# A transformer trunk on one core: another beat for the attention pairs beside the gate sums, and other sizes for the modulation sums

## The chip, the core and the metric

The kernel runs on one core of a Trainium2 chip. Its engines work side by side and wait for each other only by semaphores: TensorE (PE in the profile; PEld is its loading of weights), VectorE (DVE), ScalarE (ACT), GpSimd (POOL) and SyncE (SP), which starts most transfers. The metric is the device time of one execution in microseconds (us), lower being better.

## The reference

One layer of a hybrid backbone, in fp32, on 128 context tokens and 256 latent tokens of width 2048 (16 heads of 64):

```python
def trunk_layer(x, cond, lw, attend):
    ...
    sh1, sc1, g1, sh2, sc2, g2 = modulation(cond, w_mod_l, b_mod_l)
    h = rms_norm(x, n1) * (1 + sc1) + sh1
    q, k, v, u = project_in(h, w_in_l, qg_l, kg_l)
    attn = attend(q, k, v)
    x = x + g1 * token_mixing(h, attn, u, w_na_proj_l, w_fnet_proj_l, w_gate_l, w_o_l)
    h2 = rms_norm(x, n2) * (1 + sc2) + sh2
    x = x + g2 * swiglu(h2, w_gu_l, w_down_l)
    return x, k, v

def modulation(cond, w_mod, b_mod):
    m = jax.nn.silu(cond) @ w_mod + b_mod
    return jnp.split(m[..., None, :], 6, axis=-1)

def token_mixing(h, attn, u, w_na_proj, w_fnet_proj, w_gate, w_o):
    ...
    na = attn.reshape(b, t, D_NA) @ w_na_proj
    fn = fourier_mix(u) @ w_fnet_proj
    g_na, g_fn = jnp.split(jax.nn.sigmoid(h @ w_gate), 2, axis=-1)
    return (g_na * na + g_fn * fn) @ w_o
```

Context tokens attend to themselves; latent tokens attend in one softmax to a window of their grid and to 128 cached keys. `fourier_mix` is the real part of a 2-D DFT over positions and group channels.

## The kernel before

All large products are made in three passes: a number is split into a rounded part H and a rest L, and `mm3` issues H x H, H x L and L x H (lines 145 to 147; for the weights, `split` casts H on ScalarE at line 141 and subtracts L on VectorE at line 142). Weights come in units of 2 x 128 rows by 512 columns. `next_unit` hands PE the next unit, splits the unit two later, and lets side work advance. Nothing is scheduled by the compiler: every engine runs its instructions in the order in which the code writes them.

Side work is written as generators under `Paced`: one `yield` is one step, a rate says how many steps a tick takes. The list `behind` gets one tick per weight unit; the list `front` gets three, two in `next_unit` and one in `mid_unit`, which is called in the middle of a unit, between its second and third slice of 128 features.

The stages that matter here:

1. Input projection (512-wide matmuls). The modulation sums `mod_sums` make shift and scale of the first norm: `MODS` lists sums as (first k-tile, number n of k-tiles), each of 8 steps whose matmuls (line 402, 128 x n columns wide) take four column groups of PE at once; then `mod_cols` turns the rows into columns (line 418), and `modulate` makes H and L of each of these k-tiles of the layer's input (`hH`, `hL`). Their weights `wm` have four buffers. The projection goes through groups of k-tiles, `GROUPS` = 1, 2, 4 and 9, each over all eight column blocks, and needs a k-tile's `hH` and `hL` when its group starts on it. `PREP` are the rates of the modulation work in each group, `DUE` its first advance. When the modulation is through, `rows` begins: the other modulation rows, added up on VectorE (`accr`, line 327).
2. Gate sums (384-wide matmuls): eight sums `fc8`, each of 8 weight units with four accumulators of 128 features. After the last unit, each accumulator is copied out into `gst` (line 1029), and the four are stored by ScalarE's queue (line 1032). Beside them, three ticks a unit, `front` runs the Fourier part and then attention, eight pairs of heads. One pair's ticks are the fields of `PAIR`, divided by commas: qk transposes queries and keys and splits them; b adds the mask to the bias; s0 and s1 are the scores of each half of the queries, m their maxima, e the exponentials, i the reciprocals and scalings, t the transposes of the probabilities, v the split of the values, pv the product with the values of the pair before; lq, lv, lb load the next pair's data. A sum has 24 ticks, a pair 15.
3. Gate products, output projection, feed-forward.

The accumulators (PSUM) are two pools of four tiles: `mm` and `at`. `acc_tile` takes them from a ring of seven, three of `at` and four of `mm`; side work takes `at` tiles (after the output projection, `mm` tiles) beside the ring. `new_ring` starts it anew, last before the gate products.

Ahead of the change, the copy of the first two accumulators goes to VectorE where one of the last three ticks had exponentials, else to ScalarE:

```python
(nc.vector.tensor_copy if f < 2 and any(soft) else nc.scalar.copy)(st, po[f][:, :TOK])
```

Of the kernel before, what the change touches and what calls it, by code (L numbers as in the profile page):

```python
# [29 lines left out]
TOK = CTX + LAT  # L30
# [5 lines left out]
HALF = NL + NC  # L36


MODS = [(0, 1), (1, 3), (4, 3), (7, 3), (10, 3), (13, 3)]
GROUPS = [(0, 1), (1, 2), (3, 4), (7, 9)]  # L40
ORDER = [6, 7, 0, 1, 2, 3, 4, 5]
DUE = [-1.4, 0, 0, 0]
PREP = [1.75, 1.8, 1.8, 1.8]
PAIR = "qk,b,pv,s0 m0,e0 i0,lq,s1 m1,e1 i1,,t0 lb,v,,t1,lv,"

# [52 lines left out]
def trunk_kernel(ctx: ExitStack, tc: tile.TileContext, io: dict):  # L100
    nc = tc.nc
# [89 lines left out]
    front, behind = [], []  # L191
# [10 lines left out]
    def mid_unit():  # L202
        for p in front:
            p.tick()
# [59 lines left out]
    with ExitStack() as ph:  # L264
# [3 lines left out]
        def mm_tile():  # L268
            return ps.tile([P, CH], F32, tag="mm", name=nm("mm"))
# [3 lines left out]

        ring = None

        def new_ring():

            nonlocal ring
            ring = itertools.cycle([at_tile] * 3 + [mm_tile] * 4)

        def acc_tile():

# [87 lines left out]
        def depth_of(n):  # L370

            return 4 if n == 1 else 2

        def mod_weights(alloc):
# [12 lines left out]

            return Ahead(load, [(kt0, n, k0) for kt0, n in MODS for k0 in range(0, KT, depth_of(n))], 0)

        def mod_sums(src, kt0, n, alloc, out):  # L390


            w, nk = n * P, depth_of(n)
            pm = at_tile()
            for k0 in range(0, KT, nk):
                _, wm = src.take()
                for kk in range(0, nk, 2):
                    for ty in range(2):
                        for par in range(2):
                            k = k0 + kk + par  # L400
                            q = 32 * (2 * ty + par)
                            nc.tensor.matmul(  # L402
                                pm[q : q + 32, :w], csz[:, k, :], wm[:, ty, kk + par, :],
                                start=k < 2, stop=k >= KT - 2, tile_position=(0, q), skip_group_check=True,
                            )
                    if kk + 2 >= nk:
                        src.more()
                    if k0 + kk + 2 >= KT:
                        rows = alloc([P, w], "mrow")
                        nc.scalar.copy(rows, pm[:, :w])  # L410
                        out.append(rows)
                    yield
# [22 lines left out]
        with ExitStack() as pha:  # L435
# [117 lines left out]
            sums = []  # L553
            for i, _ in enumerate(mod_sums(src, *MODS[0], wme, sums)):
                if i in (1, 3, 5):
# [5 lines left out]
            def columns_and_tokens(k0, n):  # L561
                yield from mod_cols(k0, n, sums.pop(0))
                for kt in range(k0, k0 + n):
                    modulate(kt)
                    prepared[0] = kt + 1
                    yield

            def prepare():

                follow = columns_and_tokens(*MODS[0])  # L570
                while prepared[0] < 1:
                    yield next(follow)
                for k0, n in MODS[1:]:
                    for _ in mod_sums(src, k0, n, wme, sums):
# [75 lines left out]
            for gi, (k0, n) in enumerate(GROUPS):  # L650
                prep.due, prep.rate = DUE[gi], PREP[gi]
                if gi == len(GROUPS) - 1:
                    behind.append(Paced(expand_rpb()))
                    new_ring()
                for rate, ci in zip(CHUNKS, ORDER):
                    if gi == len(GROUPS) - 1:
                        rows.rate = rate
                    po = [(mm_tile if gi < len(GROUPS) - 1 else acc_tile)() for _ in range(NT)]
# [35 lines left out]
        def fourier():  # L694
            with ExitStack() as st:
# [60 lines left out]
                    i = slice(4 * pair + cp, 4 * pair + cp + 3, 2)  # L756
                    split(fHs[:, i], fLs[:, i], f)

                for _ in range(6):
                    yield  # L760
                lat = table([P, 2, 2 * NL], io["dft_lat"].rearrange("(t p) n -> p t n", p=P))
                ctx_ = table([P, 256], io["dft_ctx"])
# [47 lines left out]
                values()  # L810

        qks, vs, biases = [], [], []
        soft = deque(maxlen=3)

        def load_qk(hp):
            ci, co = hp // 4, (hp % 4) * P
# [26 lines left out]
        def attention_pair(hp, wk, values_before):  # L843
# [152 lines left out]
            }  # L996
            for tick in PAIR.split(","):
                for w in tick.split():
                    work[w]()
                soft.append("e" in tick)  # L1000
                yield
            return values

# [11 lines left out]
        for fc8 in range(8):  # L1015
            po = [mm_tile() for _ in range(4)]
            sts = []
            for u in range(0, KT, 2):
                wH, wL = next_unit()
                for f in range(4):  # L1020
                    s = slice(f * P, (f + 1) * P)
                    if f == 2:
                        mid_unit()
                    for kk in range(2):
                        k = u + kk
                        mm3(po[f][:, :TOK], wH[:, kk, s], wL[:, kk, s], hH[k], hL[k], k == 0, k == KT - 1)
                    if u == KT - 2:
                        st = gst.tile([P, TOK], F32, tag="st", name=nm("gst"))
                        (nc.vector.tensor_copy if f < 2 and any(soft) else nc.scalar.copy)(st, po[f][:, :TOK])  # L1029
                        sts.append(st)  # L1030
            for f, st in enumerate(sts):
                nc.scalar.dma_start(s_gate[fc8][:, f], st)
# [36 lines left out]
                    gates.more()  # L1069
                yield  # L1070

        new_ring()
        for f4 in range(4):
            gl = [None, None]
            for i, bH, bL in ((1, fH, fL), (0, aH, aL)):
                _, gl[i] = gates.take()
                po = [acc_tile() for _ in range(4)]
# [84 lines left out]
    for cc in range(4):  # L1162
        xin[cc] = tmp.tile([P, NT, CH], F32, tag="xin", name=nm("xin"))
        behind.append(Paced(load_residual(cc)))
        po = [acc_tile() for _ in range(NT)]
# [121 lines left out]
    for part, nf in enumerate(FF_PARTS):  # L1287
# [5 lines left out]
        for c4 in range(nf // 4):  # L1293
            for half in (1, 0):
                po = [acc_tile() for _ in range(4)]
# [35 lines left out]
        for cc in range(4):  # L1331
            po = [acc_tile() for _ in range(NT)]
# [72 lines left out]
```

## Time and profile before

| | |
|---|---|
| median of three runs | 2059.26 us (2057.69 to 2059.97) |
| the profiled execution | 2057.84 us, its span 2056.0 us |
| PE busy | 2030.4 us, 99% of the span |
| VectorE, ScalarE busy | 1247.9 us (61%), 758.2 us (37%) |
| moved by DMA | 390.46 MB, mean 190 GB/s |
| granted clock of TensorE | 0.998 |

Busy time of PE counts a matmul from its start to its modelled end, and matmuls overlap: two 384-wide ones start 0.17 us apart and last 0.33 each. So PE reads as busy where it is slowed down, and its stalls are found in the list of waits and in distances between matmuls. In a timeline, the columns are start, length, engine, line, operation, tiles written and read, count, and in brackets the idle time before with what ended it. In the list of waits they are engine, tile and line that waited, what for, and then total us, times, and the longest. The input projection runs until about 330 us, the gate sums until about 683, gate products until about 815, the output projection until about 950.

### The profile page before, as it was taken

To read this page: it belongs to the slowest core of one execution; us is meant where nothing else is said; L and a number is where in the kernel's file an instruction comes from. 1 tells how busy PE (TensorE), PEld (TensorE's weight loads), DVE (VectorE), ACT (ScalarE), POOL (GpSimd) and SP (SyncE) were. 2 spreads that over 40 slices of the span, in tenths; PEclk is the share of its full clock that TensorE was granted. 3 is DMA by queue.
4 is the path that set the end of the run, shared out by engine and by line. 5 is a ranking of instruction groups with operands and counts; after the bars stand their busy time and mean duration, and the time that the engine had idled before them with its cause. 6 is when DMAs were issued, how large, how long until landed. Compare 5 with 4: busy or idle time off the path is not lost.

```text
span 2056.0 us, 27530 instructions
## 1 busy us (share of the span) xinstructions
PE 2030.4 (99%) x10986; PEld 1843.9 (90%) x10986; DVE 1247.9 (61%) x1528; ACT 758.2 (37%) x1135; POOL 43.1 (2%) x92
## 2 busy tenths in 40 slices
PE   7999999999999999999999999999999999999999
PEld 4668788999989999788998999899989998999897
DVE  4746988778887777765855454454454434333456
ACT  4433232456656433334533332223322232233222
POOL 1000000000001000010000000000000000000000
PEclk9999999999999999999999999999999999999999
DMA  9996978776776776755455555455554444444453
GB/s 326 350 318 205 324 232 302 231 210 209 228 207 180 268 241 200 240 165 157 130 155 153 164 154 159 140 153 161 157 158 139 124 124 132 124 132 123 133 164 123
DMA packets 220384, 390.46 MB, mean 190 GB/s; under 512 B 28464, under 2 KB 77632, under 8 KB 220256
## 3 DMA queue, kind: packets, MB, share of 16 engines
q1 hardware_dynamic: 213088, 382.13, 59.0%
q10 hardware_dynamic: 4672, 6.31, 0.8%
q8 instruction: 86, 1.41, 0.3%
q0 software_dynamic: 2496, 0.27, 0.1%
q14 instruction: 42, 0.34, 0.1%
HBM read 371.81 MB, written 20.51 MB: 191 GB/s over the span
## 4 chain that ended last, share of the span: by engine, by line
PE 90%; DVE 3%; DMA 3%; ACT 2%; issue 1%; SPq 1%; DVEq 0%; ACTq 0%
PE mm L145 18%; PE mm L146 18%; PE mm L147 18%; PE at L145 11%; PE at L147 11%; PE at L146 11%; DMA wm<-in_w_mod 1%; PE at L402 1%; DVE accr L327 1%; DVE wl L142 1%; DMA wmr<-in_w_mod 1%; ACT wh L141 1%; PE at L336 0%; PE at L955 0%; PE at L976 0%
## 5 line engine op out<-in xcount | busy, mean ns | idle before, releaser
L142 DVE TENSOR_TENSOR wl<-wraw,wh 128x1024 fp32r<-128x1024 f32 (+1 forms) x464 | 559.5, 1206 | 672.7 <-ACT wh L141 671.8
L141 ACT CAST wh<-wraw 128x1024 fp32r<-128x1024 f32 (+1 forms) x464 | 481.4, 1039 | 1035.2 <-PE mm L146 360.4
L145 PE MATMUL mm<-hH,wh 128*128 128x384 f32 x1232 | 416.3, 338 | 5.8 <-DVE gst L1029 4.3
L147 PE MATMUL mm<-hH,wl 128*128 128x384 f32 x1232 | 412.2, 335 | 0.0
L146 PE MATMUL mm<-hL,wh 128*128 128x384 f32 x1232 | 412.0, 334 | 0.0
L327 DVE SCALAR_TENSOR_TENSOR accr<-wmr,csz,accr 128x1024 f32<-128x1024 f32 x240 | 305.2, 1280 | 3.3 <-DMA wmr<-in_w_mod 3.2
L145 PEld LDWEIGHTS mm<-hH,wh 128*128 128x128 f32 x1232 | 231.3, 188 | 12.4 <-DVE gst L1029 4.8
L146 PEld LDWEIGHTS mm<-hL,wh 128*128 128x128 f32 x1232 | 231.4, 188 | 0.0
L147 PEld LDWEIGHTS mm<-hH,wl 128*128 128x128 f32 x1232 | 231.2, 188 | 0.0
L147 PE MATMUL at<-hH,wl 128*128 128x384 f32 x560 | 187.1, 334 | 0.0
L145 PE MATMUL at<-hH,wh 128*128 128x384 f32 x560 | 187.1, 334 | 0.0
L146 PE MATMUL at<-hL,wh 128*128 128x384 f32 x560 | 187.1, 334 | 0.0
L145 PE MATMUL mm<-wh,hH 128*128 128x512 f32 x388 | 155.9, 402 | 1.3 <-ACT hH L546 1.2
L146 PE MATMUL mm<-wl,hH 128*128 128x512 f32 x388 | 152.3, 393 | 0.9 <-DVE wl L142 0.8
L147 PE MATMUL mm<-wh,hL 128*128 128x512 f32 x388 | 152.1, 392 | 0.4 <-DVE hL L142 0.4
L147 PE MATMUL mm<-wh,cL 128*128 128x512 f32 x312 | 121.6, 390 | 0.0
L146 PE MATMUL mm<-wl,cH 128*128 128x512 f32 x312 | 121.5, 389 | 0.0
L145 PE MATMUL mm<-wh,cH 128*128 128x512 f32 x312 | 121.5, 389 | 0.0
L146 PEld LDWEIGHTS at<-hL,wh 128*128 128x128 f32 x560 | 105.1, 188 | 0.2
L145 PEld LDWEIGHTS at<-hH,wh 128*128 128x128 f32 x560 | 105.1, 188 | 0.2
L147 PEld LDWEIGHTS at<-hH,wl 128*128 128x128 f32 x560 | 105.1, 188 | 0.0
L145 PEld LDWEIGHTS mm<-wh,hH 128*128 128x128 f32 x388 | 73.2, 189 | 28.8 <-issue 5.0
(283 smaller groups left out, 2705.8 us busy)
## 6 DMA issues: line engine op xcount, KB each, us to landing
wraw<-in_w_gate_up SPq DMA_DIRECT2D x176, 512.0 KB, 3.7
wmr<-in_w_mod SPq DMA_DIRECT2D x128, 512.0 KB, 4.9
wraw<-in_w_down SPq DMA_DIRECT2D x88, 512.0 KB, 3.7
wraw<-in_w_gate SPq DMA_DIRECT2D x64, 512.0 KB, 4.2
wm<-in_w_mod SPq DMA_DIRECT2D x80, 384.0 KB, 5.8
wraw<-in_w_in SPq DMA_DIRECT2D x56, 512.0 KB, 6.4
wraw<-in_w_o SPq DMA_DIRECT2D x32, 512.0 KB, 4.5
wraw<-in_w_fnet_proj SPq DMA_DIRECT2D x16, 512.0 KB, 4.9
```

The source lines that it names most:

```text
L141: nc.scalar.copy(H, x)
L142: nc.vector.tensor_sub(L, x, fr(H))
L145: nc.tensor.matmul(out, aH, bH, start=start, stop=False)
L146: nc.tensor.matmul(out, aH, bL, start=False, stop=False)
L147: nc.tensor.matmul(out, aL, bH, start=False, stop=stop)
L327: nc.vector.scalar_tensor_tensor(out=acc[:, cnd], in0=wm, scalar=sc, in1=acc[:, cnd], op0=ALU.mult, op1=ALU.add)
L402: nc.tensor.matmul(pm[q : q + 32, :w], csz[:, k, :], wm[:, ty, kk + par, :], start=k < 2, stop=k >= KT - 2, tile_position=(0, q), skip_gro ...
```

## The change

Two tables of numbers and what hangs on them. The modulation sums go in blocks of 1, 2, 2, 2, 3, 3, 3 k-tiles, where they were 1, 3, 3, 3, 3, 3; the rates in the later groups are 2.2, 2.0, 2.0 instead of 1.8. `PAIR` has 16 ticks in another order, so that a pair's place at the end of a gate sum (24 ticks) takes two values only; the Fourier part waits one tick more before it starts; all copies of gate accumulators go to ScalarE; the ring before the gate products starts with one `mm` tile.

```diff
-MODS = [(0, 1), (1, 3), (4, 3), (7, 3), (10, 3), (13, 3)]
+MODS = [(0, 1), (1, 2), (3, 2), (5, 2), (7, 3), (10, 3), (13, 3)]
...
-PREP = [1.75, 1.8, 1.8, 1.8]
-PAIR = "qk,b,pv,s0 m0,e0 i0,lq,s1 m1,e1 i1,,t0 lb,v,,t1,lv,"
+PREP = [1.75, 2.2, 2.0, 2.0]
+
+
+PAIR = "qk,b,s0 m0,e0 i0,pv,lq v,,t0,,,s1 m1,e1 i1,lv,lb,,t1"
...
-        def new_ring():
+        def new_ring(behind=0):
...
-            ring = itertools.cycle([at_tile] * 3 + [mm_tile] * 4)
+            ring = itertools.cycle([mm_tile] * behind + [at_tile] * 3 + [mm_tile] * (4 - behind))
...
-                for _ in range(6):
+                for _ in range(7):
                     yield
...
-        soft = deque(maxlen=3)
...
-                soft.append("e" in tick)
...
-                        (nc.vector.tensor_copy if f < 2 and any(soft) else nc.scalar.copy)(st, po[f][:, :TOK])
+                        nc.scalar.copy(st, po[f][:, :TOK])
...
-        new_ring()
+        new_ring(1)
```

Three places on ScalarE, in the order of the built programs. The first is where the third group of k-tiles starts (k-tiles 3 to 6). `wh` is the cast of a weight unit, `mrow` the copy of a modulation sum's rows, `hf` and `hH` the modulated k-tile, its number right behind the name. Before, where `wh210` is the first unit that meets k-tile 6:

```order
L141 CAST hH5_203_956<-hf205_958 128x384
L141 CAST wh210_989<-wraw174_813 128x1024
L550 ACTIVATE hf215_1002<-xT19_206,msh0_112,msc0_110 128x128
L550 ACTIVATE hf215_1002<-xT19_206,msh0_112,msc0_110 128x256
L141 CAST hH6_213_1000<-hf215_1002 128x384
L141 CAST wh221_1040<-wraw185_865 128x1024
```

and now, where the first unit that meets it is again one named `wh210`, which stands two rows ahead of these:

```order
L143 CAST wh221_1051<-wraw187_880 128x1024
L552 ACTIVATE hf227_1074<-xT19_206,msh0_112,msc0_110 128x128
L552 ACTIVATE hf227_1074<-xT19_206,msh0_112,msc0_110 128x256
L143 CAST hH5_225_1072<-hf227_1074 128x384
L143 CAST wh229_1099<-wraw198_931 128x1024
L552 ACTIVATE hf234_1112<-xT19_206,msh0_112,msc0_110 128x128
L552 ACTIVATE hf234_1112<-xT19_206,msh0_112,msc0_110 128x256
L143 CAST hH6_232_1110<-hf234_1112 128x384
```

K-tile 6 stood right behind the cast of the unit that meets it; it now stands behind the casts of the two units after that one.

The second is the end of the sixth gate sum. `sc` are scores and probabilities, `gst` the copies. Before (the first two copies are on VectorE, only their stores are seen here):

```order
L907 ACTIVATE sc_5421<-at_5568,rq 128x128
L907 ACTIVATE sc_5421<-at_5569,rq 128x128
L141 CAST wh_5582<-wraw_5346 128x1024
L929 ACTIVATE sc_5421,sm_5586<-sc_5421,mx_5580 128x384 x2
L939 ACTIVATE sc_5421<-sc_5421,sm_5586 128x384 x2
L1029 COPY gst_5619<-mm_5112 128x384
L1029 COPY gst_5627<-mm_5113 128x384
```

and now:

```order
L864 ACTIVATE qH_5555<-at_5546,qg_81 128x384
L870 ACTIVATE kH_5559<-at_5550,qg 128x384
L871 CAST kH_5559<-at_5550 128x128
L143 CAST wh_5568<-wraw_5364 128x1024
L1029 COPY gst_5581<-mm_5144 128x384
L1029 COPY gst_5589<-mm_5145 128x384
L908 ACTIVATE sc_5545<-at_5591,rq 128x128
L912 ACTIVATE sc_5545<-at_5591,rq 128x128
L908 ACTIVATE sc_5545<-at_5592,rq 128x128
L912 ACTIVATE sc_5545<-at_5592,rq 128x128
L1029 COPY gst_5621<-mm_5146 128x384
L1029 COPY gst_5629<-mm_5147 128x384
```

The exponentials and scalings (lines 929 and 939) are gone from ahead of the copies; the splits of queries and keys and the reading of the scores stand there.

The third is the end of the fifth gate sum. Before:

```order
L1029 COPY gst_5096<-mm_4632 128x384
L1029 COPY gst_5104<-mm_4633 128x384
L1032 DMA s_gate_95<-gst_5080 128x384
L1032 DMA s_gate_95<-gst_5088 128x384
L1032 DMA s_gate_95<-gst_5096 128x384
L1032 DMA s_gate_95<-gst_5104 128x384
L863 ACTIVATE qH_5124<-at_5115,qg_81 128x384
```

and now:

```order
L908 ACTIVATE sc_4889<-at_5109,rq 128x128
L908 ACTIVATE sc_4889<-at_5110,rq 128x128
L1029 COPY gst_5130<-mm_4654 128x384
L1029 COPY gst_5138<-mm_4655 128x384
L1032 DMA s_gate_95<-gst_5099 128x384
L1032 DMA s_gate_95<-gst_5107 128x384
L1032 DMA s_gate_95<-gst_5130 128x384
L1032 DMA s_gate_95<-gst_5138 128x384
L930 ACTIVATE sc_4889,sm_5148<-sc_4889,mx_5121 128x384 x2
L940 ACTIVATE sc_4889<-sc_4889,sm_5148 128x384 x2
```

Behind the four stores stood the split of the next pair's queries; now the exponentials and scalings of the second half stand there.

## The prediction

> **What bounds the kernel now.** I read the page first, then the list of waits, then the timeline at each place where TensorE (PE) stands still.
>
> ```profile
> span 2056.0 us, 27530 instructions
> PE 2030.4 (99%) x10986; PEld 1843.9 (90%) x10986; DVE 1247.9 (61%) x1528; ACT 758.2 (37%) x1135; POOL 43.1 (2%) x92
> ...
> L141 ACT CAST wh<-wraw 128x1024 fp32r<-128x1024 f32 (+1 forms) x464 | 481.4, 1039 | 1035.2 <-PE mm L146 360.4
> ```
>
> The second row gives each engine's busy time, the third the cast that ScalarE (ACT) makes of every weight unit (1.04 us). PE is idle for 25.6 us of 2056.0, so no change of order can win more than that plus what hides in stretched matmuls. The execution itself took 2057.84 us, 1.84 us beside its span and 1.42 us below the median of 2059.26. The sum is made against 2057.84, and 1.42 is added for the median.
>
> ```profile
> PE mm L145 <- DVE gst L1029: 4.3, 2, 2.7
> PE mm L145 <- ACT gst L1029: 1.6, 1, 1.6
> ```
>
> The first matmul of a gate sum waits three times, 5.9 us together, for the copy that empties the accumulator of the sum before. The worst of the three, after the sixth sum:
>
> ```profile
> 592.42 1.04 PE L955 MATMUL at<-ident,sc 128*128 128x128 f32 x8
> ...
> 594.37 1.26 DVE L327 SCALAR_TENSOR_TENSOR accr<-wmr,csz,accr 128x1024 f32<-128x1024 f32 x1
> ...
> 595.52 0.84 ACT L1029 COPY gst<-mm 128x384 f32<-128x384 f32 x2
> 595.55 1.02 DVE L1029 COPY gst<-mm 128x384 f32<-128x384 f32 x2
> ...
> 596.16 0.45 PE L145 MATMUL mm<-hH,wh 128*128 128x384 f32 x1 [2.70 <-DVE gst L1029]
> ```
>
> The sum's last matmul stands just ahead of the transposes at 592.42, yet both engines copy only from 595.5, since exponentials (on ScalarE) and a modulation row (on VectorE, DVE) stood ahead in their queues. The second place is the start, where the weights of the second modulation sum (three k-tiles) come late. I measure a visit to the modulation sums as the distance between the two projection matmuls around it, less their own spacing of 0.23.
>
> ```profile
> 32.15 0.39 PE L147 MATMUL mm<-wh,hL 128*128 128x512 f32 x1
> ...
> 33.25 0.50 PE L145 MATMUL mm<-wh,hH 128*128 128x512 f32 x1
> ...
> 35.20 0.39 PE L147 MATMUL mm<-wh,hL 128*128 128x512 f32 x1
> ...
> 38.53 0.50 PE L145 MATMUL mm<-wh,hH 128*128 128x512 f32 x1
> ...
> 40.48 0.39 PE L147 MATMUL mm<-wh,hL 128*128 128x512 f32 x1
> ...
> 43.41 0.50 PE L145 MATMUL mm<-wh,hH 128*128 128x512 f32 x1
> ...
> 45.37 0.39 PE L147 MATMUL mm<-wh,hL 128*128 128x512 f32 x1
> ...
> 48.85 0.48 PE L145 MATMUL mm<-wh,hH 128*128 128x512 f32 x1
> ...
> 60.85 0.39 PE L147 MATMUL mm<-wh,hL 128*128 128x512 f32 x1
> ...
> 62.60 0.50 PE L145 MATMUL mm<-wh,hH 128*128 128x512 f32 x1
> ```
>
> One step alone costs 0.87 (32.15 to 33.25), two cost 1.52 (60.85 to 62.60): 0.22 a visit and 0.65 a step, and 0.11 more because the next matmul starts slower. At 35.20 two steps cost 3.10, at 40.48 2.70; at 45.37 one step and the column products cost 3.25 where the row below makes about 0.87 + 0.83 and a wait for their rows (some 0.6, which stays) expectable. The late weights cost 1.6 + 1.2 + 0.9 = 3.7 us, most of it inside matmuls that count as busy.
>
> ```profile
> 80.07 0.83 PE L418 MATMUL at<-sel,mrow 128*128 128x4 f32 x6
> 22.17 0.63 PE L402 MATMUL at<-wm,csz 128*32 128x128 f32 x12 [0.29 <-DMA wm<-in_w_mod]
> ```
>
> **The modulation sums.** The steps go from 40 (five sums of 8, 384 wide) to 48: 24 at 384 and 24 at 256. The 256-wide step is not in this trace. Its ends are two thirds of the 384-wide one (0.43, if width alone sets it) and the 384-wide one itself, 0.65. The 128-wide step took at most 0.42 (8 of the 12 records above, the last one's drain counted in), well under 0.65, so width sets most of it and I take 0.45. The sums then cost 24 x 0.45 + 24 x 0.65 - 40 x 0.65 = +0.4 us; the ends make this -0.1 and +5.2, and the 128-wide step speaks for the lower half. The built order has 25 visits where there were 23, +0.7; one more group of column products, +0.5. The higher rates (2.2 and 2.0) move a sum's end: k-tile 6 is now made only after the weight split of two units later, which waits for PE to end the unit before. From that end ScalarE needs a cast (1.04), two activations and a cast, about 2.4 us; PE reaches the tile after two steps (1.5) and three matmuls (0.7), about 2.3: +0.3 with VectorE's part, from 0 to 1.2. The modulation rows behind start one unit later; they are VectorE work ahead of its need, so I cost that at nothing (its cover is VectorE's idle 39%; without it one accumulation, 1.28).
>
> Against this stands what comes sooner. Until its last step the second sum needs 4.2 MB instead of 6.3 MB.
>
> ```profile
> 5.00:20.00 15.00, 10.95 (x73) 9.42 (x77) 9.93 (x26) 11.28 (x30) 1.80 (x4) 0.93 1.06 306
> 30.00:60.00 30.00, 28.08 (x143) 16.06 (x140) 15.65 (x27) 17.60 (x31) 0.00 (x0) 1.00 1.06 378
> ```
>
> At the 378 GB/s (last column) of 30 to 60 us that is 5.5 us sooner; at the 306 of the earlier stretch, where pieces of 512 bytes run, 4.2/0.306 against 6.3/0.378 is 2.9 sooner. PE's own visits shrink too, by 8 x 0.2, so it asks sooner by that and by the waits. I let 0.4 of the 3.7 stay (0 to 2). Start: -3.7 + 0.4 + 0.4 + 0.7 + 0.5 + 0.3 = -1.3 us, from -3 to +2.
>
> [...]
>
> **The gate sums.** A gate sum has eight weight units of three ticks, 24 ticks; a pair now has 16, so its phase at a sum's end alternates between two values, the first pair starting one tick later (seven waits instead of six in the Fourier part). At every end the first two copies now stand on ScalarE with no exponentials ahead of them: the last long ScalarE work (the casts after a half's transposes) is two or three ticks old. PE needs the first accumulator only after the other two slices' 12 matmuls (2.1 us) and the scores, and a copy takes about half a us. The three waits go: -5.9 us. What is late next:
>
> ```profile
> 547.88 0.49 PE L857 MATMUL at<-ident,qp 128*128 128x128 f32 x3
> ...
> 548.14 1.90 ACTq L1032 DMA_DIRECT2D s_gate<-gst  x4
> 550.08 0.58 ACT L863 ACTIVATE qH<-at,qg 128x384 fp32r<-128x384 f32 x1 [1.53 <-issue]
> ```
>
> After the fifth sum, which ended at 547.88, the four stores of gate rows hold ScalarE's queue until 550.08, 2.2 us. After sums 3, 5 and 7 the new order has the second half's exponentials and scalings right behind these stores.
>
> ```profile
> 537.29 0.62 ACT L929 ACTIVATE sc<-sc,mx 128x384 f32<-128x384 f32 x1
> ...
> 538.83 1.13 ACT L939 ACTIVATE sc<-sc,sm 128x384 f32<-128x384 f32 x2 [0.23 <-DVE sm L937]
> ```
>
> ```profile
> 589.65 0.33 PE L147 MATMUL mm<-hH,wl 128*128 128x384 f32 x1
> ...
> 592.25 0.34 PE L147 MATMUL mm<-hH,wl 128*128 128x384 f32 x1
> ```
>
> That work takes 2.67 (537.29 to 539.96), so it ends 4.9 us after the sum. PE gets to its transposes after 24 matmuls of 0.173 (15 spacings in 2.60 above), 4.3 us: it waits 0.6 there, three times, +1.8 (0 to 4, if VectorE puts a 1.28 accumulation ahead of the reciprocal). After sums 4 and 6 it is the first half's exponentials: ready about 4.3 + 3.5 = 7.8 after the scores, wanted after 12 matmuls, the values and 24 matmuls, about 8.4; a 1.28 in the way makes it 0.7 late, so +0.3 each, +0.6. The scores follow the transposes of queries and keys by 12 matmuls in five of eight pairs, by a unit before:
>
> ```profile
> 436.21 0.49 PE L857 MATMUL at<-ident,qp 128*128 128x128 f32 x3
> ...
> 438.51 0.28 DVE L875 TENSOR_TENSOR kL<-at,kH 128x128 fp32r<-128x128 f32 x1
> ```
>
> The split keys are ready 2.58 after the transposes start; the scores would start after 1.03 + 2.1 + 0.1 = 3.2. That fits, and with 1.28 in VectorE's way is 0.7 late: +0.1 a pair, +0.5 (0 to 3.5). The last pair's values stand in the last tick, 12 matmuls nearer their transposes: +0.1. Loads of bias tiles come four ticks (7 to 8 us) before use instead of seven; VectorE alone would wait, its cover is the two units by which weight splits lead. New waits: +3.0 (0 to 6). Gates: -2.9.
>
> **The accumulators.** The ring of seven now starts with one mm tile. 44 tiles are taken until the first feed-forward sum, 44 mod 7 = 2, so that sum takes at, at, mm, mm instead of at, mm, mm, mm. The transposes beside it, which take mm tiles, had one buffer and now have two.
>
> ```profile
> 962.02 0.51 PE L1208 MATMUL mm<-ident,r 128*128 128x128 f32 x3 [0.30 <-DVE vL L1155]
> 963.11 0.55 PE L1149 MATMUL mm<-ident,x 128*128 128x128 f32 x3 [0.57 <-ACT rB L1209]
> ```
>
> Both waits are for that one buffer: -0.9 (0 to -1.1). The gate products take other tiles in the same number; nothing there waits for one now, and I cost it at nothing.
>
> **Sum.** -1.3 - 2.9 - 0.9 = -5.1: 2052.7 for an execution like the profiled one, 2054.2 as a median.
>
> **Rivals.** (a) No new waits: then -8.1, 2051.2 as a median. For it: ScalarE is 37% busy. Against: the row at 548.14. [...] (b) The waits only move: attention's chains eat the 5.9, -2.2 remains, 2057.1. For it: VectorE is busy 43.77 us of 50 in this stage (third figure of the row), and every chain lost a tick.
>
> ```profile
> 500.00:550.00 50.00, 48.41 (x306) 46.81 (x305) 43.77 (x58) 33.65 (x78) 0.00 (x0) 1.00 0.75 217
> ```
>
>  (c) Slower: the second half's chain, from scores to scaled probabilities, has five ticks instead of six.
>
> ```profile
> 446.64 0.44 PE L890 MATMUL at<-kH,qH 64*128 64x384 f32 x2
> ...
>
> ```
>
> ```profile
> 618.80 0.44 PE L890 MATMUL at<-kH,qH 64*128 64x384 f32 x2
> ...
>
> ```
>
> In the first pair it took 9.6 us, in the seventh 6.4. In six pairs PE now comes back after 0.7 + 36 x 0.173 + 0.1 = 7.0. If it stays 9.6, PE waits 2.6 six times, 15.6: 2057.84 - 8.1 + 15.6 + 1.42 = 2066.8. It decides above 7.0 + 8.1/6 = 8.4 us. Against: the long ones had the first half's exponentials ahead on ScalarE, which now end four ticks sooner. (d) The change does not do what it says: that the copies don't come free is excluded by the ticks, which are counted, not timed; it gets no chance. (e) The smaller tiles run at a lower rate and stay as late as the larger: the 3.7 us stay but for the 0.4 already kept, 3.3 more than the forecast, 2057.5. For it: 306 GB/s where 256 KB pieces ran. Against: those had rows of 512 bytes, the new ones have 1 KB.
>
> **Chances.** What a measurement of this kernel can tell from no change is about 0.2%, 4.1 us. Forecast (4.1 to 7 us won) 0.40, (a) 0.20, (b) 0.28, (e) 0.06, (c) 0.06: faster 0.60, same 0.34, slower 0.06. The range 2050.5 to 2058.5 takes in (a) at 2051.2, (b) and (e), and leaves out (c) and some 0.1 at the edges; the forecast's own is 2052.2 to 2055.1.
>
> **What would show it.** No wait for gst at the column ends; PE waits at the probability transposes of pairs 1, 4 and 7 near 0.6 us, named ACT sc; visits of 1.1 us for two 256-wide steps and no stretched ones before 50 us; no wait at L1208 or its like. Wrong if PE waits for qL or kL at the scores, or if the transposes wait in more than three pairs.

## The result, and the profile after

The changed kernel takes 2081.5 us in the median of four runs (2079.4 to 2082.7), the kernel before 2059.6: a ratio of 1.0107, 95% interval 1.0089 to 1.0124. It is 22 us slower where 5 us faster was forecast. The head of the page and four lines of the list of waits (engine, tile and line that waited, for what, total us, times, longest):

```profile
span 2080.2 us, 27680 instructions
...
PE 2040.7 (98%) x11050; PEld 1849.6 (89%) x11050; DVE 1248.8 (60%) x1527; ACT 760.8 (37%) x1140; POOL 43.2 (2%) x92
```

```profile
PE at L956 <- ACT sc L940: 11.2, 16, 1.9
PE at L338 <- DVE accr L329: 3.9, 2, 2.1
PE at L891 <- DVE kL L876: 2.4, 4, 0.8
PE mm L147 <- ACT gst L1029: 0.8, 1, 0.8
```

The waits for accumulators fell from 5.9 to 0.8 us, as forecast. In their place stands the first line: TensorE waits for the scaled probabilities, 11.2 us. PE is idle for 39.5 us, 13.9 more than before, and busy for 10.3 more. The stages, each from the first matmul of one to that of the next in the timelines (us):

| | input projection | gate sums | gate products | output projection | feed-forward |
|---|---|---|---|---|---|
| before | 334.3 | 345.5 | 134.4 | 138.5 | 1103.3 |
| changed | 332.4 | 368.9 | 139.0 | 137.6 | 1102.2 |

The start won 1.9 and the two stages behind the gate products 0.9 and 1.1; the gate sums lost 23.4 and the gate products 4.6. Part of this is no wait at all. In the changed kernel's timeline, behind the wait of the eighth pair,

```profile
688.27 0.34 PE L149 MATMUL mm<-hH,wl 128*128 128x384 f32 x1
...
690.51 0.33 PE L956 MATMUL at<-ident,sc 128*128 128x128 f32 x1 [1.90 <-ACT sc L940]
...
692.29 0.52 PE L147 MATMUL mm<-hH,wh 128*128 128x384 f32 x1
692.61 0.52 PE L148 MATMUL mm<-hL,wh 128*128 128x384 f32 x1
```

the matmuls stand 0.32 apart (692.29 to 692.61), where they are 0.17 apart elsewhere. The busy times of two stretches show why: first the stretch and its length, then busy us of PE, PEld, DVE, ACT and POOL, then PEclk, the granted clock.

```profile
688.50:691.91 3.41, 1.33 (x9) 1.03 (x9) 2.50 (x4) 2.31 (x6) 0.00 (x0) 1.00 0.24 52
691.91:695.33 3.42, 3.42 (x13) 3.42 (x12) 3.40 (x5) 0.98 (x3) 0.00 (x0) 0.51 0.97 304
```

For 3.41 us the clock was half (0.51). Between its start and its last 3 us the changed kernel has four such intervals (473.5, 562.2, 691.9 and 784.1 us), the kernel before none. One costs about 1.55 us: four kernels below (e7_halves_swap, e8_stores, e13_pv, e17_new15) have the changed kernel's wait in the gate products but no such interval there, and 137.5 us instead of 139.0.

The same view beside attention, before and then changed:

```profile
440.00:675.00 235.00, 229.15 (x1463) 219.06 (x1462) 196.22 (x261) 145.72 (x328) 9.72 (x20) 1.00 0.69 205
```

```profile
440.00:675.00 235.00, 219.21 (x1345) 203.95 (x1344) 176.27 (x235) 137.71 (x310) 9.71 (x20) 0.99 0.67 193
```

VectorE (the third busy time) and ScalarE (the fourth) are both less busy than before, and get through fewer instructions in the same time (235 against 261, and 310 against 328). Their work has hardly grown (1248.8 and 760.8 us over the whole span, 1247.9 and 758.2 before), and neither is busy all the time; they wait for each other more. From the lists of waits in these 235 us, before and then changed:

```profile
ACT sc L907 <- DVE sc L902: 29.9, 8, 5.0
DVE wl L142 <- ACT wh L141: 1.7, 5, 0.6
```

```profile
ACT sc L908 <- DVE sc L903: 65.4, 15, 6.0
DVE wl L144 <- ACT wh L143: 15.7, 12, 2.7
```

ScalarE's reading of the scores waits for VectorE's into the same tile, with casts queued behind it; VectorE's weight splits wait for those casts. From the second half's scores to its scaled probabilities the eight pairs take 8.9, 5.8, 11.4, 10.4, 8.6, 11.4, 8.1 and 9.6 us, 9.3 on average; before it was 8.1. TensorE also comes back to them sooner. The first pair before, and the seventh in the changed kernel, from the scores (line 890, now 891) to the transposes (955, now 956):

```profile
446.64 0.44 PE L890 MATMUL at<-kH,qH 64*128 64x384 f32 x2
...
456.69 0.82 PE L955 MATMUL at<-ident,sc 128*128 128x128 f32 x6
```

```profile
650.10 0.44 PE L891 MATMUL at<-kH,qH 64*128 64x384 f32 x2
...
657.70 0.33 PE L956 MATMUL at<-ident,sc 128*128 128x128 f32 x1 [0.37 <-ACT sc L940]
```

Before, the transposes start 10.05 us behind the scores in five of the eight pairs, later in the others, and none of them waits. In the changed kernel TensorE is ready for them after 7.1 us in four pairs (the start of the matmul ahead of them, and the usual 0.17), and in the seventh, shown here, it waits. A chain of the old average length would already be late.

### The profile page after: what moved, and what is told of

Read it like the earlier page. It is cut to its first block, busy times and chain, and to the rows that moved or that the text cites. A ratio compares the mean times of both kernels' runs of the same rounds, so it can differ in the third digit from the quotient of the medians.

```text
span 2080.2 us, 27680 instructions
## 1 busy us (share of the span) xinstructions
PE 2040.7 (98%) x11050; PEld 1849.6 (89%) x11050; DVE 1248.8 (60%) x1527; ACT 760.8 (37%) x1140; POOL 43.2 (2%) x92
## 4 chain that ended last, share of the span: by engine, by line
PE 68%; DVE 1%; ACT 1%; issue 0%; DMA 0%; ACTq 0%; SPq 0%; DVEq 0%
PE mm L147 13%; PE mm L148 13%; PE mm L149 13%; PE at L147 10%; PE at L149 10%; PE at L148 10%; DVE accr L329 1%; DVE wl L144 0%; PE at L338 0%; DMA bp<-s_rpb 0%; PE at L1149 0%; DMA wmr<-in_w_mod 0%; ACT sc L930 0%; DVE pt L144 0%; PE at L956 0%
## 5 line engine op out<-in xcount | busy, mean ns | idle before, releaser
L147 PE MATMUL mm<-hH,wh 128*128 128x384 f32 x1152 | 391.3, 340 | 0.8 <-ACT gst L1029 0.8
L149 PE MATMUL mm<-hH,wl 128*128 128x384 f32 x1152 | 387.6, 336 | 0.0
L148 PE MATMUL mm<-hL,wh 128*128 128x384 f32 x1152 | 387.0, 336 | 0.0
L147 PE MATMUL at<-hH,wh 128*128 128x384 f32 x640 | 213.9, 334 | 0.0
L149 PE MATMUL at<-hH,wl 128*128 128x384 f32 x640 | 213.9, 334 | 0.0
L148 PE MATMUL at<-hL,wh 128*128 128x384 f32 x640 | 213.8, 334 | 0.0
L149 PE MATMUL mm<-wh,cL 128*128 128x512 f32 x352 | 137.0, 389 | 0.0
L148 PE MATMUL mm<-wl,cH 128*128 128x512 f32 x352 | 137.0, 389 | 0.0
L147 PE MATMUL mm<-wh,cH 128*128 128x512 f32 x352 | 136.9, 389 | 0.0
L147 PEld LDWEIGHTS at<-hH,wh 128*128 128x128 f32 x640 | 120.1, 188 | 1.0 <-ACT wh L143 0.8
```

The source lines that it names most:

```text
L147: nc.tensor.matmul(out, aH, bH, start=start, stop=False)
L148: nc.tensor.matmul(out, aH, bL, start=False, stop=False)
L149: nc.tensor.matmul(out, aL, bH, start=False, stop=stop)
```

## The experiments

Gate sums are given from each profile; times are medians against the kernel before run beside them.

**Which part loses: e1_start, e2_gate.** The two halves of the change, each put alone into the kernel before.

```diff
 # e1_start
+MODS = [(0, 1), (1, 2), (3, 2), (5, 2), (7, 3), (10, 3), (13, 3)]
+PREP = [1.75, 2.2, 2.0, 2.0]
 # e2_gate
+PAIR = "qk,b,s0 m0,e0 i0,pv,lq v,,t0,,,s1 m1,e1 i1,lv,lb,,t1"
+                for _ in range(7):
+                        nc.scalar.copy(st, po[f][:, :TOK])
```

> The kernel before with the new sizes and rates of the modulation sums alone. The changed kernel reached its first gate matmul 1.9 us sooner than the kernel before (332.44 against 334.34), and in it a modulation row's products waited twice for VectorE (1.78 and 2.09 us), the second with a half-clock interval behind it (about 1.6). Theory A (those two waits belong to the gate part, where VectorE's queue has grown): the time is 1.9 us under before, no wait for accr. Theory B (they belong to this part, because the rows now start later against the weight units): -1.9 + 3.9 + 1.6, that is 3 to 4 us over before, with both waits there.

> The kernel before with the gate part alone: the new order of a pair, its later start, and all copies of gate accumulators on ScalarE; the old sizes of the modulation sums and the old ring. If the loss sits in the gate part, as the stages of the changed kernel say (gate sums 368.9 us where they were 345.5), this is 20 to 24 us slower than before, with TensorE's waits at the transposes of the probabilities near 11 us. If the parts only do this together, it is less than 10 us slower.

e1_start: 2060.5 us, ratio 1.0002 (0.9993 to 1.0011). The start won its 1.9 and the gate products lost 4.5:

```profile
759.60 1.06 PE L336 MATMUL at<-accr,ones 128*32 128x512 f32 x4 [2.10 <-DVE accr L327]
760.59 0.69 PE L145 MATMUL at<-fH,wh 128*128 128x384 f32 x1
761.08 0.53 PE L146 MATMUL at<-fL,wh 128*128 128x384 f32 x1
761.40 0.53 PE L147 MATMUL at<-fH,wl 128*128 128x384 f32 x1
```

In this timeline the row's products meet an accumulation that is not done and wait 2.10 us, and the half clock follows (the matmuls from 761.08 on stand 0.32 apart). Theory B holds for the second of the two waits; the first, in the gate sums, is absent here, and so the time stays short of the 3 to 4 us over that B gave. e2_gate: 2080.5 us, 1.0100 (1.0085 to 1.0114), gate sums 368.1: the gate part makes the loss by itself.

**VectorE's share and the order of the halves: e4_rows, e3_halves.**

```diff
 # e4_rows
-RATES = [1.5, 0.5, 1.1, 0.937, 0.452]
+RATES = [1.5, 0.25, 1.9, 1.6, 0.452]
 # e3_halves
+PAIR = "qk,b,s0 m0,e0 i0,pv,lq v,s1 m1,e1 i1,t0,,,,lv,lb,,t1"
```

> The changed kernel with the modulation rows at half their pace beside the gate sums (0.25 a tick instead of 0.5; 1.9 and 1.6 a unit in the two stages behind instead of 1.1 and 0.937), which takes some 48 accumulations of 1.28 us off VectorE there. To be read in the gate sums alone. Theory V: the second half's chain shortens from 9.3 us on average to about 7.5, TensorE's waits at the transposes fall from 11.2 us to 2 or less, and the gate sums from 368.9 us to about 355. Theory S: chains and waits stay within 2 us of the changed kernel's. For the whole time: about 2067 by V, if the stages behind have room for the rows.

> The changed kernel with the second half's scores moved from tick 10 to tick 6 of the 16, its exponentials from 11 to 7, and the first half's transposes from 7 to 8, so that VectorE no longer has the first split of probabilities ahead of the second half's scores and TensorE comes back nine ticks later instead of five. Theory V (the chain from the second half's scores to the scaled probabilities is long because VectorE reads the scores behind a split of probabilities, accumulations and weight splits): the waits at the second half's transposes go, -9 us and two or three half-clock intervals of 1.6 with them, about 2067. Theory S (ScalarE's queue makes it long: four stores of 1.9 us, copies, exponentials): the waits go to the first half's transposes or to the copies of the accumulators, and the time stays over 2075. Theory L (16 ticks with this phase lose in themselves): over 2075 too, with the waits at scores and copies.

e4_rows: gate sums 344.3 us, 24.6 less than in the changed kernel. Its list of waits has those at the transposes nearly gone:

```profile
PE at L338 <- DVE accr L329: 6.7, 2, 3.5
...
PE at L956 <- ACT sc L940: 1.6, 7, 0.5
```

Work taken off VectorE shortens the second half's chains, to 7.8 us on average. The whole is still 2078.6 us: the rows now weigh on the stages behind (147.4 and 150.3 us where it was 139.0 and 137.6). e3_halves went the wrong way: 2092.5 us, gate sums 378.4. Theories S and L had it over 2075 with waits at the copies of accumulators, though not 11 us slower than the changed kernel: TensorE waited 8.0 us for these copies, and the second half's chains took 11.4 us.

**ScalarE's queue: e5_swap, e6_before_swap, e7_halves_swap, e8_stores.** In three, ScalarE's reading is issued ahead of VectorE's, so that it waits for TensorE alone (in the changed kernel, in the kernel before, in e3_halves). In the fourth GpSimd starts the gate stores.

```diff
 # e5_swap, e6_before_swap, e7_halves_swap, for each of the two heads
+                    nc.scalar.activation(out=sc[...], in_=o[:, LAT:TOK], func=AF.Copy, scale=r)
                     nc.vector.scalar_tensor_tensor(out=sc[...], in0=o[:, :LAT], scalar=r, ...)
-                    nc.scalar.activation(out=sc[...], in_=o[:, LAT:TOK], func=AF.Copy, scale=r)
 # e8_stores
-                nc.scalar.dma_start(s_gate[fc8][:, f], st)
+                nc.gpsimd.dma_start(s_gate[fc8][:, f], st)
```

> The changed kernel with one exchange inside the scores: ScalarE's readings of the scores (the columns of the last window part and of the context) are issued ahead of VectorE's. Now each of ScalarE's readings waits until VectorE's reading into the same tile is done (70.9 us of waits, against 29.9 before), and the casts of weights, copies of accumulators and stores queue behind it; VectorE in turn waits for those casts. Theory P (the two queues hold each other up): with the exchange ScalarE waits for TensorE alone, 70.9 falls below 15, VectorE's waits for casts beside attention (15.7 us between 440 and 675) fall below 5, TensorE's waits at the transposes from 11.2 to 4 or less, the gate sums from 368.9 us to 350 to 357, the time to about 2066. Theory V (VectorE's own backlog makes the chain, whoever waits behind it): the gate sums stay above 363, the time above 2076.

> The kernel before with the same exchange alone. Theory P: here eight of the sixteen readings wait (29.9 us), so there is less to win: the copies of the accumulators behind them come sooner where that was their trouble, gate sums 345.5 to about 343, 0 to 3 us faster. Theory V: no change, within 1 us. If the exchange moves VectorE's queue back (VectorE now waits for ScalarE at the scores), 2 to 5 us slower.

> The changed kernel with the halves close together (second half's scores at tick 6, its exponentials at 7, first transposes at 8), which took 2092.5 us, and the exchange. In it TensorE waited 8.0 us for the copies of accumulators, which stood behind ScalarE's waiting readings of the scores. Theory P: those waits go, the order of the halves is then free to help, gate sums from 378.4 us to about 350, time about 2062. Theory V: gate sums stay above 368.

> The changed kernel with the four stores of gate rows after each sum started by GpSimd instead of ScalarE. Theory S (the 1.9 us that they hold ScalarE's queue ahead of the second half's exponentials make the chain late, as the forecast had it): TensorE's waits at the transposes of pairs 1, 4 and 7 (three after sums 3, 5 and 7: 1.21, 1.58 and the like) shorten by 1 us or more each, the time by 4 to 6. Theories P and V: the stores cost what the forecast said, 0.6 a place, and the time falls by at most 2.

e5_swap: 2072.4 us, 9 less than the changed kernel; gate sums 359.0, no half-clock interval in them. From its list of waits:

```profile
PE at L956 <- ACT sc L940: 6.0, 15, 1.0
```

That is half of what theory P asked for. ScalarE's wait only moved on: beside attention it now waits 32.0 us for the maxima. In the kernel before the exchange does nothing (1.0003, 0.9993 to 1.0014). e7_halves_swap: 2083.1 us, gate sums 373.7, short of P: 6.9 of the 8.0 us of waits for copies stay, so they were not only the doing of the waiting readings. e8_stores: 2074.2 us, 7.3 less than the changed kernel, of which 5.4 in the gate sums and 1.55 a half-clock interval that no longer fell into the gate products. The stores cost more than the 1.8 forecast. The waits at the second transposes of pairs 1, 4 and 7 shorten by 1.4, 1.1 and 0.6 us, and those of pairs 5 and 8 grow by 0.7 and 0.4. Each theory is half right, and none says why the same work fitted before.

**More ticks, and single steps moved: e9_late, e13_pv, e14_v.** e9_late turns the second half's probabilities in tick 1 of the next pair.

```diff
 # e9_late (the last pair's transposes follow after its ticks)
+PAIR = "qk,b t,s0 m0,e0 i0,pv,lq v,,t0,,,s1 m1,e1 i1,lv,lb,,"
 # e13_pv
+PAIR = "qk,b,pv,s0 m0,e0 i0,lq v,,t0,,,s1 m1,e1 i1,lv,lb,,t1"
 # e14_v
+PAIR = "qk,b,s0 m0,e0 i0,pv,lq,,t0,,v,s1 m1,e1 i1,lv,lb,,t1"
```

> The changed kernel with the second half's transposes moved on by two ticks, into tick 1 of the next pair (its product with the values stays at tick 4), so that the chain from the second half's scores has seven ticks instead of five. Theory C (the chain takes 9.3 us because of both queues, and the new order gives it five ticks of about 2 us less what TensorE needs itself): TensorE's waits at the second half's transposes, 11.2 us in the changed kernel, fall to 1 or less and the half-clock intervals in the gate sums (three of about 1.6 us) go with them; gate sums from 368.9 us to 350 to 355, time about 2066. Theory P (the two queues hold each other up and the wait only moves): it comes back at the copies of accumulators and at the values, gate sums above 362.

> The changed kernel with the product with the values moved back ahead of the scores (tick 2, as in the old order; first half's scores at 3, exponentials at 4). Theory O1 (VectorE stands behind the copy lo, which stands on ScalarE behind the exponentials and scalings): VectorE's wait for lo (9.1 us between 440 and 675, 0.4 before) goes, the queue is about 2.3 us ahead at four of the pairs, TensorE's waits at the second half's transposes fall from 11.2 to 5 or less, gate sums from 368.9 us to 355 to 360, time about 2070. If it is not this step: within 3 us of the changed kernel's 2081.5.

> The changed kernel with the split of the values at tick 9 instead of 5, behind the first half's transposes, where the old order had it. Theory O2 (it is one of the works that stand in both queues between the halves; 0.62 and 0.69 us): 0 to 3 us won, waits at the second transposes stay above 8 us. If the early split is what matters: more than 8 us won.

e9_late: 2079.9 us, gate sums 366.7. The waits at the transposes fell to 3.5 us and came back at the next scores (4.6 for qL) and values (2.0 for pt). e13_pv 2084.1, e14_v 2078.3: neither of these two steps alone is the cause.

**Rows and the pieces together: e10_rowgap, e11_all, e12_before_plus.**

```diff
 # e10_rowgap
                     yield
                 yield
+                yield
                 o = rows_psum["tile"]()
 # e11_all: e9_late, e5_swap, e8_stores and e10_rowgap in one
 # e12_before_plus: the kernel before, PAIR and copies kept, with the new MODS, PREP and
 # new_ring(1), e10_rowgap and e8_stores
```

> The changed kernel with one more step of pacing between the last accumulation of a modulation row and its products on TensorE. The two waits for accr (1.78 and 2.09 us) go, and with the second the half-clock interval behind it (1.55 us, by two other runs which had the same wait of 2.1 and no such interval: 137.5 us of gate products against 139.0). Gate products 139.0 to about 135, gate sums down by 1.8, time 2081.5 to about 2076. If the rows' later phase puts accumulations into new places of the attention chains, the gain is less than 3.

> Everything that helped the changed kernel, together: second half's transposes two ticks later, ScalarE's readings ahead of VectorE's (9.1 us alone), gate stores from GpSimd (7.3 alone), one more step ahead of the rows' products. If the pieces remove the same waits, the gate sums end near the kernel before's 345 less its 5.9 us of waits for accumulators, 340 to 346, and the time is 2049 to 2056, below the kernel before. If 16 ticks with this order keep waits at the scores, the gate sums stay over 350 and the time over 2060.

> The kernel before, its order of a pair kept, with the new modulation sums, the new ring, one more step ahead of the rows' products, and the gate stores from GpSimd. From the stages measured: -1.9 in the input projection, -1.3 in the output projection, 0 in the gate products where the new start alone lost 4.5 us to a wait for accr and a half-clock interval; the stores off ScalarE win 0 to 3 in the gate sums. 2053 to 2056, if the rows' one step more moves nothing else.

e10_rowgap: 2076.2 us as expected, gate products back at 134.4; 2.5 us of it came back in the output projection as a wait at the rows' columns. e11_all: 2072.1 us, gate sums 358.4: all the relief together does not save the new order. e12_before_plus: **2052.3 us, ratio 0.9965 (0.9952 to 0.9977)**, faster than both kernels. Its gate sums take 340.2, with one wait for an accumulator left in its list:

```profile
PE mm L145 <- DVE gst L1030: 0.9, 1, 0.9
```

What was hoped of the new order, the old one gives once the stores are off ScalarE's queue and the rows' phase is shifted; which of the two did it was not tried apart.

**Length or order, and where the ticks fall: e15_old16, e16_plus16, e17_new15, e18_tick.** A weight unit has three ticks. Call them A (ahead of the unit's cast), B (right behind it) and C (mid-unit). Fifteen ticks are five units, so in the kernel before every pair meets the casts in the same way; with 16 each pair moves on by one.

```diff
 # e15_old16, and e16_plus16 with e8_stores and e10_rowgap: the changed kernel with
+PAIR = "qk,b,pv,s0 m0,e0 i0,lq,s1 m1,e1 i1,,t0 lb,v,,t1,lv,,"
 # e17_new15: the changed kernel with range(6) and
+PAIR = "qk,b,s0 m0,e0 i0,pv,lq v,,t0,,s1 m1,e1 i1,lv,lb,,t1"
 # e18_tick: the kernel before with
-                for _ in range(6):
+                for _ in range(7):
```

> The changed kernel with the old order of a pair and one empty tick at its end, so 16 ticks as in the new one; all else as changed. Theory O (the order inside the pair makes the loss, not the 16 ticks or their phase at a sum's end): gate sums 340 to 348 us (345.5 before), no waits at the second transposes, time 2053 to 2061. Theory L (16 ticks and their phase lose): gate sums over 355, time over 2066.

> The same (old order, 16 ticks, all copies of accumulators on ScalarE, new modulation sums and ring) with the gate stores from GpSimd and one more step ahead of the rows' products. The kernel before with these last two, the new sums and the ring took 2052.3 us with gate sums of 340.2, one wait of 0.9 for an accumulator left. Theory O: gate sums 339 to 341, time 2050 to 2053, so the 16 ticks are worth at most that 0.9. Theory L: over 2060.

> The changed kernel with one empty tick less between the first transposes and the second half's scores, so 15 ticks in the new order, started as before (six waits). Known so far: old order with 15 ticks 345.5 us of gate sums, old order with 16 ticks 359.0, new order with 16 ticks 368.9. Theory U (a pair that keeps its place against the weight units' casts and splits is what matters, and 16 ticks break it): 350 to 357 us, the order's own share of 5 to 10 staying, time 2063 to 2070. Theory O (the order alone, the length does nothing to it): 365 or more, time over 2077.

> The kernel before with one edit: the Fourier part and all eight pairs start one tick later (seven waits instead of six), so that every pair starts on the tick of a unit on which pairs 1, 4 and 7 of the old order with 16 ticks had chains of 11 to 13 us. Theory U: chains of the second half of 11 us or more in most pairs, TensorE waits at their transposes in five or more of the eight, gate sums from 345.5 us to 355 or more, time over 2067. Without it: gate sums 343 to 348, time within 3 us of the kernel before.

e15_old16: 2071.9 us, gate sums 359.0, halfway; e16_plus16: 2066.4, gate sums 354.6. In the timeline of e15_old16 the second half's transposes wait for more than 0.4 us in pairs 1, 4 and 7 only:

```profile
458.36 0.33 PE L956 MATMUL at<-ident,sc 128*128 128x128 f32 x1 [1.99 <-ACT sc L940]
...
551.99 0.33 PE L956 MATMUL at<-ident,sc 128*128 128x128 f32 x1 [1.08 <-ACT sc L940]
...
649.37 0.44 PE L956 MATMUL at<-ident,sc 128*128 128x128 f32 x2 [1.60 <-DVE pt L144]
```

Those three have their scores on tick B. e18_tick put all eight there with one edit and took **2090.4 us, ratio 1.0153 (1.0139 to 1.0167)**: 31 us for one tick, gate sums 379.1. The tick moves the pairs against the end of a gate sum too: 11.2 us of its waits are for copies of accumulators, where it was 5.9. From its list of waits:

```profile
PE mm L145 <- DVE gst L1029: 9.9, 2, 5.6
PE at L955 <- ACT sc L939: 9.0, 15, 2.0
```

The first half of one pair in the timeline of ScalarE and VectorE, in the kernel before (scores on A):

```profile
530.06 0.38 ACT L911 ACTIVATE sc<-at,rq 128x128 f32<-128x128 f32 x1
530.21 0.95 DVE L917 TENSOR_REDUCE mx<-sc 128x2 f32<-128x768 f32 x1 [0.62 <-ACT sc L907]
530.31 1.06 ACT L141 CAST wh<-wraw 128x1024 fp32r<-128x1024 f32 x1
...
531.25 0.64 ACT L929 ACTIVATE sc<-sc,mx 128x384 f32<-128x384 f32 x1
531.41 1.27 DVE L327 SCALAR_TENSOR_TENSOR accr<-wmr,csz,accr 128x1024 f32<-128x1024 f32 x1
...
532.60 1.22 DVE L142 TENSOR_TENSOR wl<-wraw,wh 128x1024 fp32r<-128x1024 f32 x1
533.74 0.17 DVE L937 RECIPROCAL sm<-sm 128x4 f32<-128x4 f32 x1
533.94 1.72 ACT L939 ACTIVATE sc<-sc,sm 128x384 f32<-128x384 f32 x4 [0.60 <-DVE sm L937]
```

and in e18_tick (on B):

```profile
546.30 0.38 ACT L911 ACTIVATE sc<-at,rq 128x128 f32<-128x128 f32 x1
546.46 0.95 DVE L917 TENSOR_REDUCE mx<-sc 128x2 f32<-128x768 f32 x1 [0.56 <-ACT sc L907]
...
547.44 0.62 ACT L929 ACTIVATE sc<-sc,mx 128x384 f32<-128x384 f32 x1 [0.76 <-DVE mx L917]
...
549.55 0.18 DVE L937 RECIPROCAL sm<-sm 128x4 f32<-128x4 f32 x1 [1.82 <-ACT sc L929]
549.65 1.25 DVE L327 SCALAR_TENSOR_TENSOR accr<-wmr,csz,accr 128x1024 f32<-128x1024 f32 x1
549.76 1.71 ACT L939 ACTIVATE sc<-sc,sm 128x384 f32<-128x384 f32 x4 [0.24 <-DVE sm L937]
551.38 1.03 ACT L141 CAST wh<-wraw 128x1024 fp32r<-128x1024 f32 x1
...
552.45 1.23 DVE L142 TENSOR_TENSOR wl<-wraw,wh 128x1024 fp32r<-128x1024 f32 x1 [1.54 <-ACT wh L141]
```

On A the cast fills ScalarE while VectorE makes the maxima, and a row's accumulation and the weight split fill VectorE while ScalarE makes the exponentials. On B both gaps stay empty (0.76 and 1.82), and the accumulation, the cast and the split come behind, where the split waits another 1.54: VectorE stands idle for 3.4 us more in one half of one pair, with its next reading of scores behind that. Over the seven kernels with the old order, the second half's chain took 8.2 us on A (36 chains, 5.8 to 10.6), 9.4 on C (6, 9.2 to 9.4) and 12.4 on B (14, 10.8 to 14.3). In the changed kernel it is 5.8, 8.6 and 9.6 on A, 8.9, 10.4 and 8.1 on C, 11.4 in both pairs on B. In the old order the halves are three ticks apart, so both stand on A; in the new one they are eight apart and never do.

e17_new15: 2082.5 us, gate sums 370.1, against theory U. Its second half stands on A in all pairs (8.7 us on average), its first on C. The chain there is about as long as before, but has five ticks as in the changed kernel, where TensorE is back after 7.1 at the soonest; the transposes wait 10.7 us, and the first matmul of a sum 5.1 for copies. So both counts matter: the tick of the unit (345.5 to 379.1 for the old order) and the ticks that a chain has. A new order whose halves stand nine ticks apart, both on A, was not tried.

## Why the prediction was wrong

- **The step that failed is "New waits: +3.0 (0 to 6)".** The waits in the gate sums rose from 5.9 to 17.8 us although 5.1 were won at the copies, so the new ones are 17.0. The term had 1.8 for the second half's transposes, in pairs 1, 4 and 7; they wait 8.7, in pairs 3, 5 and 8 too, and the first half's 2.6. It had 0.5 for late keys at the scores; they wait 2.4. These are both signs that the prediction gave for being wrong. With three half-clock intervals (4.7) and what each wait costs beyond the idle time shown (688.27 to 690.51 is 2.24, 0.17 more than the usual distance and the 1.90), the rise of 11.9 is most of the 23.4. TensorE's way from the scores back to the transposes shrank from 10.05 to 7.1 us, and the term took it that the chains of most pairs would fit. I took their lengths from pairs that all stood on tick A and reckoned the pair's place only against the end of a sum, not against the unit's cast.
- **Rival (c) is nearest to what happened**, at 0.06. Its condition, above 8.4 us, was met with 9.3, and its time of 2066.8 is still 14.7 short: it had neither the waits at the first half, the keys and the rows nor the half clock. My argument against it, that the long chains had the first half's exponentials ahead on ScalarE, did not hold: these stand seven ticks ahead of the second half's scores now, and the chains are longer. VectorE's reading comes late (ScalarE's wait for it rose from 29.9 to 65.4 us).
- **The rows, costed at nothing** with "VectorE's idle 39%" as cover, cost 4.5 us in the gate products (e1_start): an average over the span is no cover at one place.
- **The stores, 0.6 at three places**, cost up to 7.3 (e8_stores). In the changed kernel a gate store took a median of 0.40 us to start and 4.6 until it landed, and yet taking the 32 starts off the queue on which the chains depend was worth 0.35% of the time.
- **The half clock was in no term**: four intervals, about 6.2 us.
- The bias loads were to have cover; VectorE waited for them, which it did nowhere in the kernel before:

```profile
DVE bp L880 <- DMA bp<-s_rpb: 1.4, 2, 1.0
```

  No wait of TensorE names them, but the chain that ended last runs through the second of these waits to the eighth pair's transposes. What that cost was not tried.
- Two sums are a little off: the start's terms add up to -1.4, not -1.3, and 24 x 0.173 is 4.2, not 4.3. Neither changes the account.
- Right: no gate sum but one waits for copies (5.9 to 0.8). The start: two 256-wide steps cost 1.32 - 0.23 = 1.09 a visit in the changed kernel's timeline, without a stretched one at the second sum:

```profile
35.38 0.39 PE L149 MATMUL mm<-wh,hL 128*128 128x512 f32 x1
36.70 0.50 PE L147 MATMUL mm<-wh,hH 128*128 128x512 f32 x1
...
38.68 0.39 PE L149 MATMUL mm<-wh,hL 128*128 128x512 f32 x1
40.00 0.50 PE L147 MATMUL mm<-wh,hH 128*128 128x512 f32 x1
```

  The first gate matmul starts at 332.8 on average in the 16 profiles with the new sums, 334.4 in the four with the old: -1.7, forecast -1.3. So the late weights went and rival (e) is out. The ring: feed-forward takes 1102.2 in the changed kernel and 1103.3 in all five profiles with the old ring, -1.1, forecast -0.9; the two waits are gone. The output projection won 0.9 as well (137.6 against 138.5), which no term had: a third wait of the kernel before, for an at tile, is gone too.

```profile
PE at L1149 <- DVE xL L1155: 0.5, 1, 0.5
```

## What to carry to other kernels

Where side work is woven into a main loop, count its steps against the loop's own work on each queue as well as against each other: a period that is not a whole number of loop turns gives every place a different fit, and one tick cost 31 us here. Before you shorten the time that a chain between two engines has, compare it with the chain's length, and measure that at the place where it is going to stand: it depends on what other work fills the gaps. Before reordering, look for what can leave the crowded queue: the stores on GpSimd, busy for 43.2 us of 2080.2, and one step more before a product, with the sums and the ring, won 7 us.

## What the runs showed of the hardware

The clock fell behind idle times of 1.4 to 2.1 us, which I had not reckoned with. In the changed kernel's profile the four half-clock intervals last 3.41 us each and start 88.7, 129.7 and 92.2 us apart, nearly 26, 38 and 27 times that. In the 3.41 us ahead of each, PE was not busy for 1.40, 1.76, 2.08 and 2.09 us; the third holds the wait of 1.90 us shown above (688.50 to 691.91). The time not busy does not settle it alone: in the same steps of 3.41 us, 1.57 (446.19 to 449.60), 1.44 (528.11 to 531.52) and 1.66 (623.68 to 627.09) had a step at full clock behind them. In the kernel before, in such steps counted from its half-clock interval at 18.04, the 2.70 us wait that ends at 596.16 fell across two, with 1.43 and 1.27 us not busy, and the clock stayed full (the 1.00 behind POOL's figure, and no half-clock interval in the gate sums).

```profile
591.48:594.89 3.41, 1.98 (x15) 1.71 (x13) 2.81 (x5) 3.09 (x8) 0.00 (x0) 1.00 0.93 295
594.89:598.30 3.41, 2.14 (x12) 2.14 (x13) 1.68 (x3) 1.52 (x5) 0.00 (x0) 1.00 0.98 322
```
